# One mixing stage, three edits: products of f taken one size at a time, v turned in the group of a token with itself, pooling maps split a step in advance

## The chip, the core and the metric

The kernel runs on one core of one Trainium2 chip. What is compared is the device time of one execution in microseconds. TensorE is PE below, its weight loads PEld, VectorE is DVE, ScalarE is ACT, GpSimd is POOL, and SP is the engine whose queue issues the DMAs.

## The reference, cut to what matters

One decoder layer over 1024 tokens of width 1024: a feed-forward half step, a mixing stage, a second feed-forward half step, an added embedding, a last norm. The change lies in the mixing stage. There, `h @ w_in` is cut into the parts q, f, input (v below), output gate, pooling input and two merge gates. Branch A is a gated linear recurrence with 8 heads of 128 x 128 state; branch B takes trailing means over 2, 4, 8 and 16 positions in four channel groups, and maps each group by a 128 x 128 matrix.

```python
f = lb + (1.0 - lb) * sigmoid(f_r);  k = 1.0 - f;  q = silu(q_r);  v = i_r
S_t = diag(f_t) @ S_{t-1} + outer(k_t, v_t);   o_t = S_t.T @ q_t      # per head
o = rmsnorm(o) * silu(og_r);                   y_a = o @ w_branch_a
pooled = trailing_mean(u, (2, 4, 8, 16)) - u                         # per channel group
mixed = (pooled @ pool_w) * pool_scale;        y_b = mixed @ w_branch_b
y = sigmoid(ga_r) * y_a + sigmoid(gb_r) * y_b; x = x + y @ w_out
```

## The kernel before, in words

**The work of PE.** Every large product is made of three matmuls per 128 x 512 part (lines 157, 158, 159: high by high, high by low, low by high of a split operand); such a part is called a part below, and takes PE about 0.69 us. Two neighbouring column blocks of `w_in` are multiplied together by `pair` with seven products in place of eight, 28 parts in all. For that DMA brings two weight tiles `ra` and `rb` (line 149); POOL makes three sums of them (lines 90 and 93); ACT casts each of `wah`, `wsh`, `wth`, `wd` (line 118), and DVE subtracts to get the low parts `wal`, `wsl`, `wtl` (line 119). The first two products of a pair need `wah` and `wal` alone. All these weight tiles, and `ra` and `rb` themselves, take turns in the twelve slots of the tag "w". The results go from PSUM (banks pA, pB, pC) by ACT copies and DVE adds (lines 345, 355, 358, 81) to tiles `o`, then by a sigmoid (line 764 for a merge gate) and a store to DRAM. The gates of the merge are `ga_dram` and `gb_dram`.

**Heads.** `hgrn(h, half)` is the recurrence of one head over 512 tokens, as a generator that yields where a group of its small matmuls ends. Each group is: the scores of each token with itself (line 869, for `score`, `ident` picks the diagonal, line 871); the turn (transpose) of v (line 877, copied at 879); then seven levels, for distances 1 to 64, of small matmuls (line 898), each followed by a masked copy into `score` (line 902, for the two largest distances ACT copies at 910) and a product of q and k with products of f (`mul(both, both, by)`, line 87); then the turn of k (925), the state (930, 942, 944), the outputs (953, 955), their norm (959, 168, 961), and at a later time the turn of the output (969, 970), which is put into the next half by `turns`. The products of f over 2, 4, ... 128 tokens are slices of one tile `tot`.

**Interleaving.** `among` writes the parts of the pairs and the groups of `hgrn` in one order: with `GROUPS` groups per head and n parts, so many parts come before each group that both end together. Head 7 has the pair GA4 (`gate_pair(GA, 4, ...)`), then `act_b`, which loads the eight half tiles `m` of the pooling branch and splits them (tiles `mh`, `ml`), the pair GA6, and the first `branch_b`. PE executes exactly this order (it is written by hand). On the other engines, and on SP, a scheduler orders the instructions ahead of time, and each engine keeps its order. All loads and stores below go through the one queue of SP, in order; an SP instruction that waits for data holds up those behind it. Slots of a tag are handed out in the order of the program.

**Two more places.** `v_load` brings v of the next half, `v_next`, at one of the later yields of the half before; for the first half of head 0, `v_of` loads it when it is called. `act_b` sets `behind`, so that its loads are issued behind the last store or load written before them.

Of the kernel before, what the change touches and what calls it, by code (L numbers as in the profile page):

```python
# [25 lines left out]
HALF = 512  # L26
EPS = 1e-6
LEVELS = (1, 2, 4, 8, 16, 32, 64)
# [9 lines left out]
def hybrid_block(ctx: ExitStack, tc: tile.TileContext, a: dict, out: bass.AP):  # L38
# [16 lines left out]
    nc = tc.nc  # L55
# [15 lines left out]
    def bank(tag, s=None):  # L71
        return psum.tile([P, HALF], F32, tag=tag, name=name(s or tag), bufs=BANKS[tag])
# [13 lines left out]
    def mul(o, x, y):  # L86
        nc.vector.tensor_tensor(o, x, y, ALU.mult)  # L87
# [40 lines left out]
    def hilo_half(src, tag, s):  # L128

        t = t_(tag, s, F32R)  # L130
        n = src.shape[1]
        hi, lo = t[:, :n], t[:, HALF : HALF + n]
        split(src, hi, lo)
        return hi, lo
# [17 lines left out]
    def store(dst, src):  # L152
        latest[0] = nc.sync.dma_start(out=dst, in_=src).ins

    def mm3(ps, ah, al, bh, bl, first, last):
        kw = {"skip_group_check": True}
        nc.tensor.matmul(ps, ah, bh, start=first, stop=False, **kw)  # L157
        nc.tensor.matmul(ps, ah, bl, start=False, stop=False, **kw)  # L158
        nc.tensor.matmul(ps, al, bh, start=False, stop=last, **kw)  # L159

    def chunks(t, n=4):
        return [t[:, c * P : (c + 1) * P] for c in range(n)]
# [646 lines left out]
    def pool_maps():  # L809

        r = t_("h", "pwr")
        load(r.rearrange("p (g d) -> p g d", g=NG), a["pool_w"].rearrange("g c d -> c g d"))
        wh, wl = hilo_half(r, "w", "pwhl")
        while pooled:
            g, u = pooled.pop(0)
            gc = slice(g * P, (g + 1) * P)
            for half in range(2):
                ph, pl = hilo_half(u[half], "w", "pb")
                ps = bank("aux")
                mm3(ps, wh[:, gc], wl[:, gc], ph, pl, True, True)  # L820
                nc.scalar.mul(u[half], ps, pscale[:, g : g + 1])
                store(m_dram[g][half], u[half])
                yield False

    def pool_pair(g):
        got = {}
# [26 lines left out]
    def hgrn(h, half):  # L853

        qk, f = heads[h][0][half], heads[h][1][half]
        q, k = qk[:, L], qk[:, R]  # L860
        qc, kc = chunks(q), chunks(k)
        state = states.get(h)
        sc = scores[half]
        nc.scalar.activation(k, f, AF.Copy, scale=-1.0, bias=1.0)
        v = v_of(h, half)

        ps = bank("aux")
        for p_, k_, q_ in zip(chunks(ps), kc, qc):
            nc.tensor.matmul(p_, k_, q_, start=True, stop=True)
        yield  # L870
        nc.vector.copy_predicated(
            sc, ident.bitcast(U32).unsqueeze(1).to_broadcast([P, 4, P]),
            ps.rearrange("p (c t) -> p c t", c=4),
        )
        ps = bank("aux")
        for p_, v_ in zip(chunks(ps), chunks(v)):
            nc.tensor.transpose(p_, v_, ident)
        yield
        nc.scalar.copy(v, ps)
        vc = chunks(v)  # L880

        tots = {1: f}
        tot = t_("h", "tot")
        at = 0
        for hh in LEVELS:
            n = HALF // (2 * hh)
            pv = tots[hh].rearrange("p (a two) -> p a two", two=2)
            tots[2 * hh] = tot[:, at : at + n]
            mul(tots[2 * hh], pv[:, :, 0], pv[:, :, 1])
            at += n  # L890
        mul(q, q, f)
        for hh in LEVELS:
            n = 64 // hh
            ps = bank("aux").rearrange("p (c x) -> p c x", c=4)
            m = 64 if hh == 64 else P
            for c in range(4):
                right = qc[c].rearrange("p (a two h) -> p a two h", two=2, h=hh)[:, :, 1, :]
                nc.tensor.matmul(ps[:m, c, :64], kc[c][:, :m], right, start=True, stop=True)  # L898
            yield
            if hh < 32:  # L900
                s4 = sc.rearrange("p c (a two h) -> p c a two h", two=2, h=hh)[:, :, :, 1, :]
                nc.vector.copy_predicated(
                    s4,
                    masks[hh].bitcast(U16).unsqueeze(1).unsqueeze(3).to_broadcast([P, 4, n, hh]),
                    ps[:, :, :64].rearrange("p c (a h) -> p c a h", h=hh),
                )
            else:
                for a_ in range(n):
                    rows = slice(2 * hh * a_, 2 * hh * a_ + hh)
                    nc.scalar.copy(  # L910
                        sc[rows, :, 2 * hh * a_ + hh : 2 * hh * (a_ + 1)],
                        ps[rows, :, hh * a_ : hh * (a_ + 1)],
                    )

            na = HALF // (2 * hh)
            both = view(qk, hh, [[HALF - hh, 2], [2 * hh, na], [1, hh]])
            by = view(tots[hh], 0, [[1, 2], [2, na], [0, hh]])
            mul(both, both, by)

        need = 4 - half
        ps = bank("aux")
        for p_, a_ in zip(chunks(ps)[:need], kc):
            nc.tensor.transpose(p_, a_, ident)
        yield
        nc.scalar.copy(k[:, : need * P], ps[:, : need * P])
        ps = bank("aux")
        for p_, a_, b_ in zip(chunks(ps)[:need], kc, vc):
            nc.tensor.matmul(p_, a_, b_, start=True, stop=True)  # L930
        yield
        assert (h, half) in og_there
        og = load(t_("h", "og"), og_dram[h][half], True)
        og_last[0] = latest[0]
        befores = []

        for c, (s_, p_) in enumerate(zip(chunks(f), chunks(ps))):
            befores.append(state)
            if c == need:
                break  # L940
            if state is None:
                nc.vector.tensor_copy(s_, p_)
            else:
                nc.vector.scalar_tensor_tensor(
                    s_, state, tots[128][:, c : c + 1], p_, ALU.mult, ALU.add
                )
            state = s_
        states[h] = state

        ps = bank("aux")  # L950
        for c, p_ in enumerate(chunks(ps)):
            s_ = befores[c]
            nc.tensor.matmul(p_, sc[:, c, :], vc[c], start=True, stop=s_ is None)
            if s_ is not None:
                nc.tensor.matmul(p_, qc[c], s_, start=False, stop=True)
        yield
        rs = const.tile([P, 4], F32, tag="rso", name=name("rso"), bufs=2)
        for c, (o_, p_) in enumerate(zip(qc, chunks(ps))):
            nc.scalar.activation(o_, p_, AF.Square, accum_out=rs[:, c : c + 1])
        rstd(rs, rs, P)  # L960
        nc.vector.tensor_tensor(
            q.rearrange("p (c t) -> p c t", c=4), ps.rearrange("p (c t) -> p c t", c=4),
            rs.unsqueeze(2).to_broadcast([P, 4, P]), ALU.mult,
        )

        def turn():
            ps = bank("aux")
            for p_, a_ in zip(chunks(ps), qc):
                nc.tensor.transpose(p_, a_, ident)
            nc.vector.scalar_tensor_tensor(og, ps, onorm[:, h : h + 1], og, ALU.mult, ALU.mult)  # L970
            store(o_dram[h][half], og)

        turns.append(turn)


    GROUPS = 2 * 13
    turns = []

    def head(h):

        for half in range(2):
            for i, _ in enumerate(hgrn(h, half)):
                if i == 2 and turns:
                    turns.pop(0)()
                if i == 7:
                    at = 2 * h + half + 1
                    if at < 2 * HEADS:
                        v_next.append(v_load(at // 2, at % 2))
                yield
# [37 lines left out]
    def act_b():  # L1027
        behind[0] = latest[0]
        for g in range(NG):
            m = t_("q", "m")  # L1030
            for half, c in enumerate((L, R)):
                load(m[:, c], m_dram[g][half])
            m_parts.append(halves(hilo(m, "a", "m")))
        m_last, behind[0] = latest[0], None
        yield True
        behind[0] = m_last
        yield True
# [14 lines left out]
    with tc.manual_schedule(engines={nc.tensor.engine}):  # L1052
        for h in range(HEADS):
            its = more[h]() if h in more else (v_pair(h + 1), qf_pair(h + 1), og_pair(h + 1))
            among(its, head(h), (74 if h == 7 else 3 * PAIR + 4 * (h in (0, 2))))
        turns.pop(0)()
    behind[0] = og_last[0]

# [241 lines left out]
```

## Time and profile before

| | |
|---|---|
| time, median of 3 runs (lowest to highest) | 2426.27 us (2423.11 to 2428.93) |
| the profiled execution, its own time | 2433.22 us |
| its span, first to last instruction | 2431.5 us |
| granted clock of PE over the span | 0.986 |
| PE busy | 2332.4 us, 96% of the span |
| DVE, ACT, POOL busy | 1471.6, 979.2, 443.6 us |
| heads of the mixing stage in the trace | about 783 to 1440 us |

The busy shares are means over the whole span. The change is in one stage, so the stage's own rows are what to read: how long PE stands idle there, what it waits for, and at which clock it runs after such a wait. Lines of "waits" name the line and tile that waits, then what ended the wait, then the sum, the number and the longest of them. A row of the timeline is start, length, engine, line, operation, output <- input, shape, count, and in brackets the idle time before it and what ended it.

### The profile page before, as it was taken

The page shows a single profiled execution, that of the slowest core. Times are in us where ns is not written, and L with a number is a line of the kernel's source. Part 1 is how long each engine was busy: PE and PEld are TensorE (multiplying, and loading weights), DVE is VectorE, ACT ScalarE, POOL GpSimd, SP SyncE. Part 2 cuts the span into 40 slices and gives each one's busy share as a digit, 9 for nine tenths or more (in the row PEclk, how much of TensorE's full clock was granted, in tenths as well). Part 3 has the DMA queues.
Part 4 walks back from the last instruction along what each step waited for, and adds up shares of the span by engine and source line. Part 5 has one row for each costly group of instructions (what it writes and reads, how often), then busy time and mean ns, then how long its engine had stood idle before and what let it go on. Part 6 is the DMA issues. An engine that isn't in the chain of part 4 may idle for free.

```text
span 2431.5 us, 29305 instructions
## 1 busy us (share of the span) xinstructions
PE 2332.4 (96%) x11003; PEld 1915.3 (79%) x11003; DVE 1471.6 (61%) x2019; ACT 979.2 (40%) x1520; POOL 443.6 (18%) x390
## 2 busy tenths in 40 slices
PE   7999999999999999999999999998999999999997
PEld 5788788888877888788888877776787888888885
DVE  5655554567656766766566566677544544568558
ACT  7533333333554333333333343247333333334655
POOL 2222222200021222122222102102222232100000
PEclk9999999999999999999999999999999999999998
DMA  5243554483332222222222267652234523664323
GB/s 191 91 160 133 179 169 143 144 328 125 118 113 70 79 95 83 74 87 78 84 91 74 87 201 243 229 195 102 96 131 141 174 97 109 237 228 133 111 95 132
DMA packets 133614, 331.21 MB, mean 136 GB/s; under 512 B 15200, under 2 KB 16224, under 8 KB 133472
## 3 DMA queue, kind: packets, MB, share of 16 engines
q1 hardware_dynamic: 133472, 329.34, 39.5%
q8 instruction: 86, 1.41, 0.3%
q14 instruction: 56, 0.46, 0.1%
HBM read 228.10 MB, written 101.19 MB: 135 GB/s over the span
## 4 chain that ended last, share of the span: by engine, by line
PE 71%; DVE 10%; DMA 7%; ACT 4%; POOL 3%; issue 3%; SPq 1%; POOLq 0%; DVEq 0%; ACTq 0%
PE pA L157 11%; PE pA L159 11%; PE pA L158 11%; PE pB L157 5%; PE pB L158 5%; PE pB L159 5%; PE aux L898 3%; PE pC L158 3%; PE pC L159 3%; PE pC L157 3%; PE aux L158 2%; PE aux L159 2%; PE aux L157 2%; DMA rb<-in_ffn_w_dram 1%; DVE qk L87 1%
## 5 line engine op out<-in xcount | busy, mean ns | idle before, releaser
L90 POOL TENSOR_TENSOR s<-rb 128x512 f32<-128x512 f32 x74 | 99.5, 1345 | 815.1 <-DMA rb<-in_ffn_w_dram 408.7
L119 DVE TENSOR_TENSOR wtl<-rb,wth 128x1024 fp32r<-128x1024 f32 x74 | 90.6, 1225 | 149.2 <-ACT wth L118 149.2
L118 ACT CAST wsh<-s 128x1024 fp32r<-128x1024 f32 x74 | 77.8, 1052 | 223.3 <-POOL s L93 210.8
L93 POOL TENSOR_TENSOR rb<-ra,s 128x512 f32<-128x512 f32 x74 | 97.2, 1314 | 352.5 <-DVE wd L119 325.8
L118 ACT CAST wth<-rb 128x1024 fp32r<-128x1024 f32 x74 | 77.7, 1049 | 184.1 <-POOL rb L93 184.1
L119 DVE TENSOR_TENSOR wsl<-s,wsh 128x1024 fp32r<-128x1024 f32 x74 | 90.7, 1226 | 99.9 <-ACT wsh L118 99.9
L898 PEld LDWEIGHTS aux<-qk 128*128 128x128 f32 (+1 forms) x896 | 110.0, 187 | 37.9 <-issue 11.1
L119 DVE TENSOR_TENSOR wal<-ra,wah 128x1024 fp32r<-128x1024 f32 x74 | 91.4, 1237 | 78.5 <-PE pC L158 45.5
L118 ACT CAST gh<-gr 128x1024 fp32r<-128x1024 f32 x84 | 81.8, 981 | 141.1 <-PE aux L158 86.3
L119 DVE TENSOR_TENSOR gl<-gr,gh 128x1024 fp32r<-128x1024 f32 x84 | 94.8, 1132 | 66.9 <-ACT gh L118 66.7
L157 PE MATMUL pA<-xT1h,wsh 128*128 128x512 f32 x280 | 115.2, 411 | 18.1 <-ACT xT1h L118 14.8
L898 PE MATMUL aux<-qk 128*128 128x64 f32 (+1 forms) x896 | 111.1, 267 | 17.1 <-DVE qk L87 8.4
L157 PE MATMUL pA<-xT3h,wth 128*128 128x512 f32 x296 | 120.0, 406 | 7.2 <-ACT g L355 7.0
L118 ACT CAST wah<-ra 128x1024 fp32r<-128x1024 f32 x74 | 77.7, 1050 | 119.2 <-DMA ra<-in_ffn_w_dram 102.1
L157 PE MATMUL pB<-xT1h,wsh 128*128 128x512 f32 x296 | 119.8, 405 | 2.7 <-DVE g L81 1.2
L157 PE MATMUL pA<-x0h,wah 128*128 128x512 f32 x296 | 118.6, 401 | 2.2 <-ACT wah L118 0.9
L157 PE MATMUL pB<-x,wth 128*128 128x512 f32 x296 | 118.3, 400 | 0.0
L157 PE MATMUL pC<-x0h,wah 128*128 128x512 f32 x296 | 118.2, 399 | 0.0
L158 PE MATMUL pB<-xT1l,wsh 128*128 128x512 f32 x296 | 117.1, 396 | 0.8 <-DVE xT1l L119 0.8
L159 PE MATMUL pB<-xT1h,wsl 128*128 128x512 f32 x296 | 117.0, 395 | 0.0
L158 PE MATMUL pA<-x0l,wah 128*128 128x512 f32 x296 | 115.9, 392 | 0.8 <-DVE x0l L119 0.8
L159 PE MATMUL pA<-x0h,wal 128*128 128x512 f32 x296 | 116.2, 393 | 0.1
(347 smaller groups left out, 6593.4 us busy)
## 6 DMA issues: line engine op xcount, KB each, us to landing
ra<-in_ffn_w_dram SPq DMA_DIRECT2D x46, 512.0 KB, 3.7
rb<-in_ffn_w_dram SPq DMA_DIRECT2D x44, 512.0 KB, 3.7
gsS<-gs SPq DMA_DIRECT2D x88, 256.0 KB, 2.1
rB<-in_ffn_w_dram SPq DMA_DIRECT2D x40, 512.0 KB, 7.0
gr<-gsS SPq DMA_DIRECT2D x40, 512.0 KB, 3.5
gsA<-g SPq DMA_DIRECT2D x66, 256.0 KB, 2.0
gr<-gsA SPq DMA_DIRECT2D x30, 512.0 KB, 5.1
ra<-in_w_in_dram SPq DMA_DIRECT2D x27, 512.0 KB, 3.6
```

The source lines that it names most:

```text
L87: nc.vector.tensor_tensor(o, x, y, ALU.mult)
L90: nc.gpsimd.tensor_tensor(o, x, y, ALU.add)
L93: nc.gpsimd.tensor_tensor(o, x, y, ALU.subtract)
L118: nc.scalar.copy(hi, src)
L119: nc.vector.tensor_tensor(lo, src, hi.bitcast(F32), ALU.subtract)
L157: nc.tensor.matmul(ps, ah, bh, start=first, stop=False, **kw)
L158: nc.tensor.matmul(ps, ah, bl, start=False, stop=False, **kw)
L159: nc.tensor.matmul(ps, al, bh, start=False, stop=last, **kw)
L898: nc.tensor.matmul(ps[:m, c, :64], kc[c][:, :m], right, start=True, stop=True)
```

## The change

`hgrn`: the transposes of v are written directly behind the matmuls of each token with itself, in the same group, so a half has eleven groups and not twelve; `mul(q, q, f)` follows at once; each product of f is written behind the level that uses the one before it. The yields at which the output's turn and the load of v are written are counted accordingly (1 and 6), and `GROUPS` goes from 26 to 24: a head of 84 parts has 3.5 parts per group, not 3.23. `pool_maps`: the split of the next map's input is written ahead of the matmuls of this one, with one more yield (and n larger by one in heads 0 and 2). `act_b`: the second and fourth tile `m` come from the tag "w" and not from "q", which spares two slots of "q".

```diff
--- before.py
+++ after.py
@@ -811,16 +811,19 @@
         r = t_("h", "pwr")
         load(r.rearrange("p (g d) -> p g d", g=NG), a["pool_w"].rearrange("g c d -> c g d"))
         wh, wl = hilo_half(r, "w", "pwhl")
-        while pooled:
-            g, u = pooled.pop(0)
+        todo = [(g, half, u[half]) for g, u in pooled for half in range(2)]
+        pooled.clear()
+        parts = [hilo_half(todo[0][2], "w", "pb")]
+        yield False
+        for i, (g, half, u) in enumerate(todo):
             gc = slice(g * P, (g + 1) * P)
-            for half in range(2):
-                ph, pl = hilo_half(u[half], "w", "pb")
-                ps = bank("aux")
-                mm3(ps, wh[:, gc], wl[:, gc], ph, pl, True, True)
-                nc.scalar.mul(u[half], ps, pscale[:, g : g + 1])
-                store(m_dram[g][half], u[half])
-                yield False
+            if i + 1 < len(todo):
+                parts.append(hilo_half(todo[i + 1][2], "w", "pb"))
+            ps = bank("aux")
+            mm3(ps, wh[:, gc], wl[:, gc], *parts.pop(0), True, True)
+            nc.scalar.mul(u, ps, pscale[:, g : g + 1])
+            store(m_dram[g][half], u)
+            yield False
 
     def pool_pair(g):
         got = {}
@@ -867,27 +870,19 @@
         ps = bank("aux")
         for p_, k_, q_ in zip(chunks(ps), kc, qc):
             nc.tensor.matmul(p_, k_, q_, start=True, stop=True)
+        pv = bank("aux")
+        for p_, v_ in zip(chunks(pv), chunks(v)):
+            nc.tensor.transpose(p_, v_, ident)
         yield
+        nc.scalar.copy(v, pv)
+        vc = chunks(v)
         nc.vector.copy_predicated(
             sc, ident.bitcast(U32).unsqueeze(1).to_broadcast([P, 4, P]),
             ps.rearrange("p (c t) -> p c t", c=4),
         )
-        ps = bank("aux")
-        for p_, v_ in zip(chunks(ps), chunks(v)):
-            nc.tensor.transpose(p_, v_, ident)
-        yield
-        nc.scalar.copy(v, ps)
-        vc = chunks(v)
 
         tots = {1: f}
         tot = t_("h", "tot")
-        at = 0
-        for hh in LEVELS:
-            n = HALF // (2 * hh)
-            pv = tots[hh].rearrange("p (a two) -> p a two", two=2)
-            tots[2 * hh] = tot[:, at : at + n]
-            mul(tots[2 * hh], pv[:, :, 0], pv[:, :, 1])
-            at += n
         mul(q, q, f)
         for hh in LEVELS:
             n = 64 // hh
@@ -916,6 +911,10 @@
             both = view(qk, hh, [[HALF - hh, 2], [2 * hh, na], [1, hh]])
             by = view(tots[hh], 0, [[1, 2], [2, na], [0, hh]])
             mul(both, both, by)
+            na, at = HALF // (2 * hh), HALF - HALF // hh
+            pv = tots[hh].rearrange("p (a two) -> p a two", two=2)
+            tots[2 * hh] = tot[:, at : at + na]
+            mul(tots[2 * hh], pv[:, :, 0], pv[:, :, 1])
 
 
 
@@ -973,16 +972,16 @@
         turns.append(turn)
 
 
-    GROUPS = 2 * 13
+    GROUPS = 2 * 12
     turns = []
 
     def head(h):
 
         for half in range(2):
             for i, _ in enumerate(hgrn(h, half)):
-                if i == 2 and turns:
+                if i == 1 and turns:
                     turns.pop(0)()
-                if i == 7:
+                if i == 6:
                     at = 2 * h + half + 1
                     if at < 2 * HEADS:
                         v_next.append(v_load(at // 2, at % 2))
@@ -1027,7 +1026,7 @@
     def act_b():
         behind[0] = latest[0]
         for g in range(NG):
-            m = t_("q", "m")
+            m = t_(("q", "w")[g % 2], "m")
             for half, c in enumerate((L, R)):
                 load(m[:, c], m_dram[g][half])
             m_parts.append(halves(hilo(m, "a", "m")))
@@ -1052,7 +1051,7 @@
     with tc.manual_schedule(engines={nc.tensor.engine}):
         for h in range(HEADS):
             its = more[h]() if h in more else (v_pair(h + 1), qf_pair(h + 1), og_pair(h + 1))
-            among(its, head(h), (74 if h == 7 else 3 * PAIR + 4 * (h in (0, 2))))
+            among(its, head(h), (74 if h == 7 else 3 * PAIR + 5 * (h in (0, 2))))
         turns.pop(0)()
     behind[0] = og_last[0]
 
```

The number of instructions of each engine is the same. What moves is shown at three places.

PE at the start of head 0 (qk_5429 is the first half's q and k, v_5946 its v; pA_5981 before and pA_5986 now are the first product of the pair that follows). Before:

```order
L159 MATMUL pA_5645<-xT3h_5731,wtl_5867 128x512
L869 MATMUL aux_5948<-qk_5429 128x128 x4
L157 MATMUL pA_5981<-x0h_5171,wah_5959 128x512
L158 MATMUL pA_5981<-x0l_5172,wah_5959 128x512
L159 MATMUL pA_5981<-x0h_5171,wal_5960 128x512
...
L159 MATMUL pA_5981<-x0h_5231,wal_5960 128x512
L877 MATMUL aux_5996<-ident,v_5946 128x128 x4
L157 MATMUL pC_5982<-x0h_5171,wah_5959 128x512
```

And now (line 872 is the old 869, 875 the old 877, 893 the old 898):

```order
L159 MATMUL pA_5645<-xT3h_5731,wtl_5867 128x512
L872 MATMUL aux_5948<-qk_5429 128x128 x4
L875 MATMUL aux_5953<-ident,v_5946 128x128 x4
L157 MATMUL pA_5986<-x0h_5171,wah_5964 128x512
L158 MATMUL pA_5986<-x0l_5172,wah_5964 128x512
L159 MATMUL pA_5986<-x0h_5171,wal_5965 128x512
...
L159 MATMUL pA_5986<-x0h_5231,wal_5965 128x512
L893 MATMUL aux_6004<-qk_5429 128x64 x4
L157 MATMUL pC_5987<-x0h_5171,wah_5964 128x512
```

The transposes of v stood behind four parts, and stand directly behind the matmuls of each token with itself. The load of v is in both orders the row directly behind the load ra of the second pair, in SP's queue.

SP near the end of head 7 (ra_10627 and rb_10633 before, ra_10633 and rb_10639 now, are the weights of the pair GA6; ga_dram_1_118 is the store of the pair GA4's last gate; og is the output gate of the second half). Before:

```order
L149 DMA ra_10627<-in_w_in_dram 128x1024
L153 DMA ga_dram_1_114_241<-o_10196 128x512
L153 DMA o_dram_1_104_231<-og_10326 128x512
L149 DMA rb_10633<-in_w_in_dram 128x1024
L153 DMA ga_dram_0_115_242<-o_10386 128x512
L153 DMA ga_dram_0_113_240<-o_10197 128x512
L153 DMA ga_dram_1_112_239<-o_10195 128x512
L153 DMA ga_dram_1_118_245<-o_10388 128x512
L149 DMA m_10595<-m_dram_0_171_298 128x512
L149 DMA m_10595<-m_dram_1_172_299 128x512
L149 DMA m_10602<-m_dram_0_173_300 128x512
L149 DMA m_10602<-m_dram_1_174_301 128x512
```

And now:

```order
L153 DMA ga_dram_1_118_245<-o_10393 128x512
L149 DMA m_10601<-m_dram_0_171_298 128x512
L149 DMA m_10601<-m_dram_1_172_299 128x512
L149 DMA m_10608<-m_dram_0_173_300 128x512
L149 DMA m_10608<-m_dram_1_174_301 128x512
L149 DMA m_10615<-m_dram_0_175_302 128x512
L149 DMA m_10615<-m_dram_1_176_303 128x512
L149 DMA m_10622<-m_dram_0_177_304 128x512
L149 DMA m_10622<-m_dram_1_178_305 128x512
L149 DMA ra_10633<-in_w_in_dram 128x1024
L149 DMA og_10908<-og_dram_1_90_217 128x512
L149 DMA rb_10639<-in_w_in_dram 128x1024
```

The load ra has moved from seven rows ahead of that store to the ninth row behind it, and rb from four rows ahead to the eleventh row behind; all eight loads of m are now ahead of both. On PE the first matmul with wah (cast from ra) stands in both orders directly behind the last product of GA4.

DVE at the same place, from the norm of half 14 on to the first levels of half 15 (qk_9771 before and qk_9776 now are its q and k, `ident` marks its first masked copy). Before:

```order
L168 TENSOR_SCALAR rso_10694<-rso_10694 128x4
L961 TENSOR_TENSOR qk_9770<-aux_10677,rso_10694 128x512
L119 TENSOR_TENSOR ml_10599<-m_10595,mh_10598 128x1024
L871 COPY_PREDICATED score_5422<-ident,aux_10703 128x512
L119 TENSOR_TENSOR ml_10606<-m_10602,mh_10605 128x1024
L81 TENSOR_TENSOR o_10623<-o_10623,pA_10651 128x512
L87 TENSOR_TENSOR qk_9771<-qk_9771,f_9773 128x512
L902 COPY_PREDICATED score_5422<-mask_73,aux_10743 128x256
```

And now:

```order
L168 TENSOR_SCALAR rso_10691<-rso_10691 128x4
L960 TENSOR_TENSOR qk_9775<-aux_10674,rso_10691 128x512
L119 TENSOR_TENSOR ml_10605<-m_10601,mh_10604 128x1024
L119 TENSOR_TENSOR ml_10612<-m_10608,mh_10611 128x1024
L879 COPY_PREDICATED score_5422<-ident,aux_10700 128x512
L119 TENSOR_TENSOR ml_10619<-m_10615,mh_10618 128x1024
L119 TENSOR_TENSOR wd_10648<-rb_10639,wd_10648 128x512
L119 TENSOR_TENSOR ml_10626<-m_10622,mh_10625 128x1024
L81 TENSOR_TENSOR o_10629<-o_10629,pA_10657 128x512
L119 TENSOR_TENSOR wtl_10654<-rb_10639,wth_10653 128x1024
L87 TENSOR_TENSOR qk_9776<-qk_9776,f_9778 128x512
L897 COPY_PREDICATED score_5422<-mask_73,aux_10727 128x256
```

The weights' wtl of GA6 stood above this piece and now stands ahead of half 15's first product with f; the products of f of half 15 stand above the piece in both.

DVE in the first half of head 1 (qk_6147 before, qk_6146 now; tot_6960 and tot_6945 are the products of f of the half that follows). Before:

```order
L902 COPY_PREDICATED score_5421<-mask_81,aux_6730 128x64x4
L87 TENSOR_TENSOR qk_6147<-qk_6147,tot_6677 128x2x64x4
L87 TENSOR_TENSOR tot_6960<-f_6150 128x256
L87 TENSOR_TENSOR tot_6960<-tot_6960 128x128
L87 TENSOR_TENSOR tot_6960<-tot_6960 128x64
L87 TENSOR_TENSOR tot_6960<-tot_6960 128x32
L81 TENSOR_TENSOR o_6428<-o_6428,pB_6549 128x512
L87 TENSOR_TENSOR tot_6960<-tot_6960 128x16
L119 TENSOR_TENSOR wsl_6835<-s_1297_6831,wsh_6834 128x1024
L902 COPY_PREDICATED score_5421<-mask_85,aux_6753 128x32x8
L87 TENSOR_TENSOR qk_6147<-qk_6147,tot_6677 128x2x32x8
```

And now:

```order
L87 TENSOR_TENSOR tot_6945<-f_6149 128x256
L897 COPY_PREDICATED score_5421<-mask_81,aux_6717 128x64x4
L87 TENSOR_TENSOR qk_6146<-qk_6146,tot_6668 128x2x64x4
L87 TENSOR_TENSOR tot_6945<-tot_6945 128x128
L87 TENSOR_TENSOR tot_6945<-tot_6945 128x64
L87 TENSOR_TENSOR tot_6945<-tot_6945 128x32
L87 TENSOR_TENSOR tot_6945<-tot_6945 128x16
L87 TENSOR_TENSOR tot_6945<-tot_6945 128x8
L87 TENSOR_TENSOR tot_6945<-tot_6945 128x4
L897 COPY_PREDICATED score_5421<-mask_85,aux_6736 128x32x8
L87 TENSOR_TENSOR qk_6146<-qk_6146,tot_6668 128x2x32x8
```

The seven products of the following half stood on both sides of the 32x8 level, with wsl ahead of it; now the six later ones stand together behind the level before it, and wsl behind the 32x8 level.

## The prediction

> **What bounds the kernel now.** I read the page first, for the engine that sets the time.
>
> ```profile
> span 2431.5 us, 29305 instructions
> PE 2332.4 (96%) x11003; PEld 1915.3 (79%) x11003; DVE 1471.6 (61%) x2019; ACT 979.2 (40%) x1520; POOL 443.6 (18%) x390
> PE 71%; DVE 10%; DMA 7%; ACT 4%; POOL 3%; issue 3%; SPq 1%; POOLq 0%; DVEq 0%; ACTq 0%
> ```
>
> PE is busy for 96%, and the chain that ended last lies on it for 71%. The number of matmuls doesn't change, so the change can win or lose only where PE stands idle or runs at a lower clock. Hence next the windows of the changed stage (stretch and its length; busy time of PE, PEld, DVE, ACT, POOL; granted clock; DMA), the whole of it and short stretches around its idle times, and then what PE waits for there.
>
> ```profile
> 783.00:1440.00 657.00, 635.59 (x3498) 534.44 (x3498) 418.93 (x716) 242.63 (x480) 137.46 (x104) 0.99 0.27 89
> 886.60:890.00 3.40, 1.97 (x13) 1.44 (x11) 2.64 (x7) 1.22 (x2) 0.00 (x0) 1.00 0.21 77
> 890.00:893.40 3.40, 3.40 (x11) 2.73 (x10) 1.02 (x2) 0.00 (x0) 0.00 (x0) 0.51 0.00 0
> 991.60:1011.00 19.40, 15.30 (x83) 12.04 (x82) 19.04 (x48) 5.02 (x9) 0.00 (x0) 1.00 0.16 54
> 1012.90:1019.70 6.80, 6.71 (x23) 5.87 (x23) 3.21 (x5) 2.42 (x4) 1.52 (x2) 0.50 0.62 220
> 1063.90:1067.30 3.40, 3.40 (x22) 3.01 (x22) 1.11 (x3) 0.00 (x0) 0.00 (x0) 1.00 0.00 0
> 1419.10:1425.90 6.80, 6.20 (x20) 5.36 (x21) 3.68 (x6) 1.79 (x3) 0.00 (x0) 0.50 0.68 237
> ```
> ```profile
> PE aux L898 <- DVE qk L87: 8.4, 13, 1.3
> PE aux L898 <- DVE tot L87: 4.2, 3, 1.4
> PE aux L898 <- ACT wb L118: 3.1, 1, 3.1
> PE aux L158 <- DVE pb L119: 2.4, 1, 2.4
> PE pA L157 <- ACT o L358: 1.1, 1, 1.1
> ```
>
> Of 657 us PE is idle for 657.00 - 635.59 = 21.4. Three stretches of 3.4, 6.8 and 6.8 us run at half the clock, each behind an idle time; half of their length is lost, 1.7 + 3.4 + 3.4 = 8.5 us. So 29.9 us is all that could be won here, 1.2% of the kernel. A third wait of about the same length as the first, 1.36 us, cost no clock (the stretch at 1063.9 has 1.00).
>
> **Products of f, one size at a time; GROUPS 24.** What a level costs DVE:
>
> ```profile
> L87 DVE TENSOR_TENSOR qk<-qk,tot 128x512 f32<-128x512 f32 x96 | 77.9, 811 | 29.3 <-PE aux L898 29.1
> L902 DVE COPY_PREDICATED score<-mask,aux 128x256 f32<-128x256 uint16 x80 | 44.3, 553 | 56.2 <-PE aux L898 56.1
> L871 DVE COPY_PREDICATED score<-ident,aux 128x512 f32<-128x512 uint32 x16 | 11.8, 737 | 0.0
> L87 DVE TENSOR_TENSOR tot<-f 128x256 f32<-128x256 f32 x16 | 9.9, 619 | 0.1
> 889.15 1.12 PE L898 MATMUL aux<-qk 128*128 128x64 f32 x8 [1.43 <-DVE tot L87]
> ```
>
> The 1.43 us ahead of 889.15 is a level whose product on DVE was late: between it and the one before stood products of f, an add and wsl. In the new order wsl is behind that level and the first product of f ahead of the level before; so the three waits on tot, 4.2 us, go, with the 1.7 us of clock behind the first. The 13 waits on qk hold 8.4 us. A part is 0.69 us, so a group of 3.5 parts instead of 3.23 covers 0.19 us more. By walking the new order with these durations I let the two longest of halves 9 and 13 go (2.8 us with what follows them), and 2.2 of the small ones; 3.4 remain, mostly in halves 1 and 5, where DVE also makes the trailing means. New waits come up: with v's group gone, only three or four parts lie between a token's scores with itself and the first level, where six or seven lay, and the chain (copy by ident, product with f, 0.74 + 0.81 us, behind other DVE work) ends 0.3 us behind PE in the even halves. I take 2.1 us for all, and 0.6 more in half 5. Between 0 and 5 us are possible: 8 halves by 0.6.
>
> Each small group also breaks the flow of large matmuls:
>
> ```profile
> 885.39 0.48 PE L157 MATMUL pA<-xT1h,wsh 128*128 128x512 f32 x1
> 885.70 0.39 PE L158 MATMUL pA<-xT1l,wsh 128*128 128x512 f32 x1
> 885.93 0.40 PE L159 MATMUL pA<-xT1h,wsl 128*128 128x512 f32 x1
> ```
>
> The first behind a group takes 0.31 us until the next starts, others 0.23. Sixteen groups fewer: 16 x 0.085 = 1.4 us. Together: -4.2 - 1.7 - 5.0 - 1.4 + 2.1 + 0.6, about -9.5 us (-5 to -13).
>
> **Maps split a step ahead.** The 2.4 us on pb, with 3.4 us of clock behind it, looks like its gain. But DVE, busy for 19.04 of the 19.40 us from 991.6 to 1011, works off means, levels and splits one after another there, and the same instructions still come before. I put it at 0: the wait moves by a group. From both sides: -5.8 if it goes, +1 if the earlier split holds up a level.
>
> **v turned at once, first half.** All other v are loaded five groups or so ahead of their half, and at 657 / 16 / 11 = 3.7 us each that is some 18 us. The first is not:
>
> ```profile
> 782.26 1.29 POOL L93 TENSOR_TENSOR rb<-ra,s 128x512 f32<-128x512 f32 x1 [4.00 <-DVE wd L119]
> 783.52 1.05 PE L869 MATMUL aux<-qk 128*128 128x128 f32 x8
> 783.58 0.33 SPq L149 DMA_DIRECT2D ra<-in_w_in_dram  x1
> 783.96 0.42 SPq L149 DMA_DIRECT2D v<-v_dram  x1
> 784.33 0.48 PE L157 MATMUL pA<-x0h,wah 128*128 128x512 f32 x1
> 787.73 0.66 PE L877 MATMUL aux<-ident,v 128*128 128x128 f32 x4 [0.42 <-DMA v<-v_dram]
> ```
>
> Its load is issued directly behind ra, which waits for a slot until POOL is done (782.26 + 1.29 = 783.55). That stays. v is there at 787.7, and PE will now ask for it at 784.33: 3.4 us idle where 0.42 was, so +2.95, and the four parts between come later. Behind 1.43 and 2.38 us of idle time the clock was halved for 3.4 and 6.8 us, so 1.7 to 3.4 us more: +4.6 to 6.4, I take 5.5. [...]
>
> **m in the tag "w", end of head 7.** This is the term that decides. E is 1399.66, where GA4's last product ends and GA6's first starts, with wah of ra.
>
> ```profile
> 1371.35 0.33 SPq L149 DMA_DIRECT2D ra<-in_w_in_dram  x1
> 1399.66 0.39 PE L157 MATMUL pA<-x0h,wah 128*128 128x512 f32 x1
> 1402.16 0.64 ACT L764 ACTIVATE o<-o 128x512 f32<-128x512 f32 x1 [0.92 <-DVE o L81]
> 1402.82 0.32 SPq L153 DMA_DIRECT2D ga_dram<-o  x1
> 1403.19 1.86 SPq L149 DMA_DIRECT2D m<-m_dram  x4
> 1409.00 1.06 ACT L118 CAST mh<-m 128x1024 fp32r<-128x1024 f32 x1 [1.08 <-DMA m<-m_dram]
> 1413.04 1.08 PE L898 MATMUL aux<-qk 128*128 128x64 f32 x8 [0.57 <-ACT o L764]
> 1419.70 1.94 PE L898 MATMUL aux<-qk 128*128 128x64 f32 x8 [3.06 <-ACT wb L118]
> ```
> ```profile
> ra<-in_w_in_dram SPq DMA_DIRECT2D x22, 512.0 KB, 3.6
> L90 POOL TENSOR_TENSOR s<-rb 128x512 f32<-128x512 f32 x22 | 29.3, 1333 | 229.2 <-DMA rb<-in_w_in_dram 186.3 <-PE aux L159 17.4 <-PE aux L925 13.7
> L119 DVE TENSOR_TENSOR wsl<-s,wsh 128x1024 fp32r<-128x1024 f32 x74 | 90.7, 1226 | 99.9 <-ACT wsh L118 99.9
> ```
>
> Before, ra was issued 28 us ahead of its use. Now it stands behind the store of GA4's last gate, which waits for that very product (copy, add, sigmoid: issued at E + 3.2 before, 2.3 by my estimate where ACT is free), and behind eight loads of m at 1.86 / 4 = 0.47 us of issue each: 2.3 + 0.3 + 3.8 = E + 6.4. Alone it would take 3.6 us, so E + 10; behind 2 MB of m it takes longer, and were it to take twice as long it would be E + 13.5; I take 11.5, nearer the fast end since m lands while ra is issued. One cast, 1.06, and PE resumes at E + 12.6. It has nothing else to do: the order is fixed.
>
> A second wait follows. The new DVE row has wal, wsl, four ml, wd and wtl ahead of half 15's first product with f. rb lands two rows later, E + 13.5; two sums on POOL (1.35 each) and a cast give wsh at 17.3; then DVE in its order: wsl 1.23, the norm of half 14 with its step on POOL 2.0, two ml 2.5, the copy by ident 0.74, ml 1.23, wd 0.7, ml 1.23, an add 0.7, wtl 1.23, the product 0.81: E + 29.7. PE gets there at 12.6 + 0.8 (wal) + nine parts 6.2 + three groups 2.7 = 22.3, up to 25 where it waits for wd. Before it was at 1413.04, E + 13.4. PE has then done three parts fewer (2.1 us), and what came next before, 3.1 us for wb, 3.4 of clock and 1.1 at 1436 (the wait on o), is mostly covered; new dips cost 1.7 to 3.4. So 29.7 + 2.1 - 13.4 - 7.6 + 2.5 = +13.3 us. The ends: with the second wait hidden and no dip +4, with slow DMAs +19.
>
> **Sum.** -9.5 + 0 + 5.5 + 13.3 = +9.3 us on the profiled 2433.2. That run lies 7 us above the median, 2426.3; put on the median it makes 2435.3 us (the likeliest one's own range 2428 to 2443).
>
> **Rivals.** (1) Only the gains: the loads are there in time, or the SP queue lets ra through. -9.5 and the old tail's waits partly gone: 2411 to 2420. For it: in every other pair ra lands long ahead. Against it: the fixed row of SP. It decides where ra is issued before E - 5. (2) Faster after all, by the maps: if the early split takes the pb wait away, -5.8 in head 2, and with a tail at its low end (+4): -9.5 - 5.8 + 5.5 + 4, 2420. Against it: DVE without a gap. (3) A draw: the first stall of the tail, its second hidden since the level's DVE work gets done meanwhile: -9.5 + 4.6 + 6, 2427. For it: PE has nine parts and three groups to do after it resumes. (4) More: both tail waits with slow m, 2445 to 2449. (5) The edits do nothing: 2426; excluded nearly by the rows of the order. (6) The clock stays full behind the first stall: without the 2.5 us for its dip, 2432.8, a case inside the forecast, about 0.1 of its 0.52, since two shorter idle times had dips.
>
> **Chances.** Forecast 0.52, (1) 0.08, (2) 0.05, (3) 0.20, (4) 0.12, (5) 0.03. A measurement can tell 0.2%, 4.9 us: bounds 2421.4 and 2431.1. Faster: (1) and (2), 0.13. Same: (3), (5) mostly 0.21. Slower: the forecast nearly whole and (4), 0.66 with what (3) reaches over. The range leaves out (1) and the upper half of (4): 2420 to 2446.
>
> **What would show it.** In the changed trace: an idle time of 3.4 us ahead of v's transposes near 784; ra of GA6 issued behind eight m; PE idle for 10 to 13 us at about 1393 for wah, then waits of 4 to 7 up to half 15's first level; no waits on tot. I am wrong if ra goes out early, if PE finds wah within 5 us, or if the chain through half 15 is hidden.

## The result, and the profile after

The change makes the kernel slower by 1.1%: 2453.4 us (median of 4 runs, 2448.4 to 2457.8) against 2425.5 us, ratio 1.0107 with a 95% interval of 1.0093 to 1.0122, so about 26 us (0.0107 times 2426). The prediction was 2435.3 us, in a range of 2420 to 2446. The direction was right; the loss is nearly three times the 9.3 us forecast.

The page after, first lines:

```profile
span 2456.1 us, 29284 instructions
PE 2334.3 (95%) x11003; PEld 1917.6 (78%) x11003; DVE 1485.6 (60%) x2019; ACT 981.4 (40%) x1520; POOL 441.1 (18%) x390
```

PE's busy time is 2 us longer than before (2332.4), its matmuls are the same in number, and the span is 24.6 us longer: in these two executions nearly all of the loss is idle time of PE. The waits of PE in the heads, up to GA6's first product (which stands at 1399.66 before and behind 1403.81 after):

```profile
PE aux L893 <- DVE qk L87: 9.5, 14, 0.8
PE aux L875 <- DMA v<-v_dram: 3.4, 1, 3.4
PE aux L158 <- DVE pb L119: 3.3, 1, 3.3
PE aux L954 <- DVE f L943: 1.3, 2, 0.7
PE aux L893 <- DVE pw L87: 1.3, 2, 0.7
PE aux L893 <- ACT f L717: 0.3, 1, 0.3
```

Without v that is 15.7 us. Before, the same stretch held 8.4 + 4.2 + 2.4 on qk, tot and pb, and 0.8 on the cast pb, together 15.8. No wait on tot is left, as forecast, but the time is not won: the same three levels, the fifth of halves 2, 6 and 10 (counted from 0), still wait 0.80, 0.79 and 0.79 us, now on qk, and new waits have come up elsewhere. The start of head 0 is as forecast too (timeline):

```profile
783.98 1.29 POOL L93 TENSOR_TENSOR rb<-ra,s 128x512 f32<-128x512 f32 x1 [3.57 <-DVE wd L119]
785.24 1.05 PE L872 MATMUL aux<-qk 128*128 128x128 f32 x8
785.29 0.33 SPq L149 DMA_DIRECT2D ra<-in_w_in_dram  x1
785.67 0.43 SPq L149 DMA_DIRECT2D v<-v_dram  x1
789.73 0.66 PE L875 MATMUL aux<-ident,v 128*128 128x128 f32 x4 [3.44 <-DMA v<-v_dram]
```

The end of head 7, in order of time (E is now 1403.81, where PE falls idle):

```profile
1405.00 0.32 SPq L153 DMA_DIRECT2D ga_dram<-o  x1
1405.37 3.76 SPq L149 DMA_DIRECT2D m<-m_dram  x8
1409.23 0.50 SPq L149 DMA_DIRECT2D ra<-in_w_in_dram  x1
...
1415.65 1.04 ACT L118 CAST wah<-ra 128x1024 fp32r<-128x1024 f32 x1 [10.68 <-DMA ra<-in_w_in_dram]
1416.75 0.80 PE L157 MATMUL pA<-x0h,wah 128*128 128x512 f32 x1 [12.94 <-ACT wah L118]
...
1424.92 0.17 DVE L168 TENSOR_SCALAR rso<-rso 128x4 f32<-128x4 f32 x1 [2.14 <-ACT qk L958]
1426.22 0.69 DVE L960 TENSOR_TENSOR qk<-aux,rso 128x512 f32<-128x512 f32 x1 [1.13 <-POOL rso L169]
1426.83 2.35 DVE L119 TENSOR_TENSOR ml<-m,mh 128x1024 fp32r<-128x1024 f32 x2
...
1431.67 2.12 POOL L93 TENSOR_TENSOR rb<-ra,s 128x512 f32<-128x512 f32 x1 [5.48 <-DVE wd L119]
...
1434.90 1.23 DVE L119 TENSOR_TENSOR wtl<-rb,wth 128x1024 fp32r<-128x1024 f32 x1 [1.64 <-ACT wth L118]
1436.04 0.68 DVE L87 TENSOR_TENSOR qk<-qk,f 128x512 f32<-128x512 f32 x1
1436.87 1.94 PE L893 MATMUL aux<-qk 128*128 128x64 f32 x8 [7.68 <-DVE qk L87]
```

The load ra goes out behind the store and eight m, PE is idle for 12.94 us, and after 12 us of work it is idle again for 7.68 us, at half 15's first level. A third wait, of 2.17 us, stands further on; before, 0.6 us were waited there:

```profile
1524.83 0.50 PE L157 MATMUL pB<-xT1h,wsh 128*128 128x512 f32 x1 [2.17 <-ACT xT1h L118]
```

Behind each of the three comes a dip, as a stretch at half the clock is called here. The windows of PE's clock (columns as in the prediction):

```profile
1405.80:1416.10 10.30, 0.00 (x0) 0.00 (x0) 0.00 (x0) 0.45 (x1) 0.00 (x0) 0.50 0.99 341
1416.10:1422.90 6.80, 6.11 (x18) 4.72 (x19) 2.45 (x2) 1.64 (x2) 3.93 (x3) 0.50 0.06 23
1422.90:1426.30 3.40, 3.40 (x23) 3.02 (x23) 0.25 (x2) 2.54 (x10) 1.02 (x1) 1.00 0.00 0
1436.50:1443.30 6.80, 6.43 (x21) 5.60 (x22) 3.33 (x6) 1.11 (x2) 0.00 (x0) 0.50 0.51 177
1525.30:1532.10 6.80, 6.04 (x15) 4.76 (x15) 4.98 (x6) 1.85 (x3) 0.00 (x0) 0.50 0.56 176
```

PE works 6.11 + 6.43 + 6.04 = 18.6 us at half the clock behind E; half of it, 9.3 us, is lost, in part where PE would have waited anyhow. Before, one dip stood there, with 6.20 us of work.

### The profile page after: what moved, and what is told of

Read it like the earlier page. It is cut to its first block, busy times and chain, and to the rows that moved or that the text cites. A ratio compares the mean times of both kernels' runs of the same rounds, so it can differ in the third digit from the quotient of the medians.

```text
span 2456.1 us, 29284 instructions
## 1 busy us (share of the span) xinstructions
PE 2334.3 (95%) x11003; PEld 1917.6 (78%) x11003; DVE 1485.6 (60%) x2019; ACT 981.4 (40%) x1520; POOL 441.1 (18%) x390
```

## The experiments

Twelve kernels, each compared with the kernel before in runs on the same chip. Its own median was 2425 to 2428 us in these comparisons, so the ratios are what to compare; 0.1% is 2.4 us.

| kernel | ratio to before | 95% interval | us, of 2426 |
|---|---|---|---|
| the change | 1.0107 | 1.0093 to 1.0122 | +26.0 |
| after_mq | 1.0025 | 1.0015 to 1.0035 | +6.1 |
| before_mw | 1.0066 | 1.0049 to 1.0084 | +16.0 |
| after_ra_first | 1.0062 | 1.0047 to 1.0076 | +15.0 |
| ra_first_q | 1.0010 | 1.0000 to 1.0020 | +2.4 |
| after_mq_v0 | 0.9996 | 0.9987 to 1.0005 | -1.0 |
| rfq_v0 | 0.9982 | 0.9971 to 0.9994 | -4.4 |
| before_tots | 1.0004 | 0.9992 to 1.0016 | +1.0 |
| before_vt_v0 | 1.0010 | 0.9999 to 1.0021 | +2.4 |
| before_pm | 1.0001 | 0.9990 to 1.0012 | +0.2 |
| v0_opm | 1.0002 | 0.9990 to 1.0013 | +0.5 |
| v0_notots | 0.9963 | 0.9951 to 0.9976 | -9.0 |
| v0_pooltots | 0.9968 | 0.9955 to 0.9980 | -7.8 |

**The tag of m, undone and alone.** The changed kernel with the old line, and the old kernel with the new line:

```diff
-            m = t_(("q", "w")[g % 2], "m")
+            m = t_("q", "m")
```

> The changed kernel with all four tiles m in the tag q again, as before; the load ra of GA6 is again seven rows ahead of the store of GA4's last gate. Theory 1 (the late ra is what costs): the idle time of 12.9 us ahead of GA6 and the one of 7.7 us at half 15's first level go, with 3.2 + 3.4 us of half clock behind them, and the old tail's waits of about 5 and 3.4 of clock come back: some 20 us less than the changed kernel, 2430 to 2435. Theory 2 (the loss is spread over the heads, in new waits of 0.5 to 0.8 us): at most 6 us less, 2447 or more.

> The kernel before with the second and fourth tile m in the tag w, nothing else. ra and rb of GA6 go behind the store and the eight loads of m here too. Theory 1: 18 to 22 us slower than before, 2444 to 2448, with an idle time of 11 to 14 us ahead of GA6's first product. Theory 2: that the late ra hurts only with the new order of the groups (four fewer), less than 8 us, under 2434.

after_mq takes 0.82% off the changed kernel, 20 us (22.7 by the medians, 2453.4 and 2430.7): theory 1. before_mw loses 0.66%, 16 us (12 to 20), a little less than expected and far more than theory 2 allows. Its waits of PE show the same two idle times as the changed kernel, 13.5 us for wah and 5.0 us at half 15's first level:

```profile
PE pA L157 <- ACT wah L118: 13.5, 1, 13.5
PE aux L898 <- DVE qk L87: 13.0, 14, 5.0
```

So this one line is worth 60 to 80% of the whole loss, in the old order of groups as in the new one.

**ra ahead of m.** In the changed kernel, ra and rb of GA6 are loaded at the start of act_b and handed to the pair; the loads of m are then issued behind rb and not behind the store:

```diff
     def act_b():
+        for s, j in (("ra", 6), ("rb", 7)):
+            ga6.append(load(t_("w", s), w_in[GA + j], True))
         behind[0] = latest[0]
```

> The changed kernel with ra and rb of GA6 loaded in act_b ahead of the loads of m; m stays in q and w by turns. The loads of m then stand behind rb and not behind the store. Theory 1 (what costs is ra standing behind the store and m): the idle time ahead of GA6 is under 1 us, 2425 to 2434. Rival (two slots fewer of w for the weights cost by themselves): PE still waits for weights of GA6 for 5 us or more, 2440 or more.

The first idle time is gone, and yet 1.0062 remains: I had expected the whole loss to go. Theory 1 is right for the first wait and wrong for the second, and part of the rival holds. Waits of PE and timeline of after_ra_first:

```profile
PE aux L893 <- DVE qk L87: 16.4, 14, 7.7
1411.75 0.62 ACT L118 CAST wd<-rb 128x512 fp32r<-128x512 f32 x1 [0.52 <-DVE ml L119]
1414.21 2.11 POOL L93 TENSOR_TENSOR rb<-ra,s 128x512 f32<-128x512 f32 x1 [5.48 <-DVE wd L119]
1419.41 1.94 PE L893 MATMUL aux<-qk 128*128 128x64 f32 x8 [7.67 <-DVE qk L87]
```

rb has been there for 20 us and more (POOL read it at 1390.28). wd waits for ml. As I read it, wd takes the slot of w that a tile m gives back when ml has read it; no row shows the slots themselves, and the next kernel tests it. The last sum of POOL waits for wd, wtl for that sum, and half 15's first product stands behind wtl on DVE. The same kernel with all m in q:

> As after_ra_first (ra and rb of GA6 loaded ahead of m), but all four tiles m in q. DVE then has wd and wtl of GA6 above the norm of half 14 again, and two ml, not four, ahead of half 15's first product. Theory (in after_ra_first the 7.7 us at half 15 came from m holding two slots of w, so that wd waited until ml had read m): that wait is 3 us or less, 2426 to 2433, as after_mq. Rival (the loads of m ahead of the store, and the order of ra and rb, caused it): a wait of 6 us or more, 2437 to 2443.

PE's waits on qk in ra_first_q:

```profile
PE aux L893 <- DVE qk L87: 10.3, 14, 1.3
```

ra_first_q is at 1.0010, and its longest wait on qk is 1.3 us in place of 7.7. So the loss of the tail has two halves: ra behind m on SP, 0.45%, 11 us (6 to 16; 1.0107 to 1.0062), and m in the slots of the weights, 0.52%, 13 us (8 to 17; 1.0062 to 1.0010). Their sum, 24 us, is the whole step from the changed kernel to ra_first_q. It is not the 20 us (16 to 24) of after_mq, since in ra_first_q the loads of m stand behind rb and not behind the store, but the intervals overlap.

**v in head 0's first half.** after_mq with one group more, in that half alone, so that the transposes of v stand behind four parts again:

```diff
+        if (h, half) == (0, 0):
+            yield
         pv = bank("aux")
```

> As after_mq, and in head 0's first half alone the transposes of v stand a group behind the scores again. Theory 1: the idle time of 3.4 us ahead of them goes back to about 0.4, with no clock to win since none was lost there: 3 us less than after_mq. Rival (the time is lost again at the next wait, since DVE or the loads set it): less than 1 us.

> As ra_first_q, with the transposes of v in head 0's first half a group later, as in after_mq_v0. Theory: 5 to 7 us less than ra_first_q (3.1 of idle time and, in most executions, a dip), 2419 to 2427; against before from 0.3% faster to the same. Rival: m's first tiles on SP hold up the stores and loads behind them, 2428 or more.

after_mq_v0 is 0.29%, 7.0 us faster than after_mq; rfq_v0 is 0.28%, 6.8 us faster than ra_first_q (each 3 to 10 us by the intervals). The wait on v is 0.3 and 0.8 us. I had expected 3 us in the first case, since the changed kernel's profile shows no half clock there. Four profiled executions hold this stall, 3.3 to 3.5 us long: the changed kernel and after_ra_first without a dip, after_mq and ra_first_q with one (the first fence is after_mq, the second ra_first_q):

```profile
784.00:787.40 3.40, 0.37 (x4) 0.18 (x2) 2.94 (x4) 1.85 (x4) 0.00 (x0) 1.00 0.72 231
787.40:790.80 3.40, 3.08 (x10) 2.60 (x11) 2.26 (x9) 1.33 (x2) 0.00 (x0) 0.50 0.21 77
```
```profile
785.40:788.80 3.40, 1.27 (x10) 1.04 (x8) 2.03 (x3) 1.71 (x3) 0.26 (x1) 1.00 0.59 174
788.80:792.20 3.40, 2.13 (x7) 1.91 (x8) 3.16 (x10) 2.09 (x3) 0.00 (x0) 0.50 0.36 134
792.20:795.60 3.40, 3.40 (x9) 2.64 (x8) 0.00 (x0) 0.00 (x0) 0.00 (x0) 0.50 0.00 0
```

One execution lost 1.5 us of clock behind this stall (half of 3.08), one 2.8 (half of 2.13 + 3.40), the two others none. With the 3 us of idle time these make 3 to 6 us; the 7 us of the ratios have these in their interval.

**Each other part alone.** before_tots, before_pm and before_vt_v0 are the old kernel with one of the change's parts as in its diff (before_vt_v0 with the extra group of head 0); v0_opm is after_mq_v0 with the old pooling maps.

> The kernel before with the products of f written one size at a time, nothing else. In the built order only DVE changes, and there only in the first half of four heads, where the product of q with f moves two or three rows ahead; the products of the other halves had been put ahead by the scheduler and stay where they were. Theory 1 (this edit does nearly nothing, and the three waits on tot stay): within 3 us of before. Theory of the prediction (the waits on tot and the dip behind them go with it): 4 to 6 us faster.

> The kernel before with v turned in the group of the scores and GROUPS 24, but in head 0's first half a group later, as before. Theory 1 (this edit alone holds what the heads win and lose; waits of 0.6 to 0.8 us at the first and fifth levels take the place of those removed): from 4 us faster to 2 us slower. Theory of the prediction (waits on tot go, first levels wait for 0.3 us each): 7 us or more faster.

> The kernel before with the pooling maps split a step in advance, nothing else. Prediction: 0, the wait on pb only moves. Rival 1 (the split goes ahead of levels that PE waits for, and the maps' first split is later by a level): 1 to 4 us slower, with the wait on pb at 3.3 us as in the changed kernel. Rival 2 (the wait on pb goes): 4 to 6 us faster.

> after_mq_v0 with the pooling maps as before, so products of f, v's turn and GROUPS alone. If the split in advance costs 1 to 4 us in the changed kernel too, this is 1 to 4 us faster than after_mq_v0, the wait on pb is 2.4 us or less, and it beats before by 0 to 5 us; if it costs nothing, the same as after_mq_v0 within 1.5 us.

None differs from before: +1.0, +2.4, +0.2 and +0.5 us, all with 1 in the interval. The products of f, written one size at a time, alone change next to nothing: PE's waits on tot in before_tots stand as they were,

```profile
PE aux L891 <- DVE tot L87: 4.1, 3, 1.4
```

since the scheduler had put them among the levels of the half before, whatever their place in the program. They go with v's turn and GROUPS, but then PE waits on qk for longer up to 1390 us, 14.8 us in before_vt_v0 where the kernel before has 8.4 on qk and 4.2 on tot:

```profile
PE aux L899 <- DVE qk L87: 14.8, 15, 3.4
```

The maps split in advance leave the wait on pb at 2.4 us where they stand alone (before_pm); with the new groups it is 3.3 us with the split (after_mq_v0) and 2.4 without (v0_opm). They cost or win nothing that these runs can tell: v0_opm is 0.06% behind after_mq_v0, within the intervals.

**Why the heads' gain went.** Two kernels on the base of after_mq_v0. v0_notots leaves out the products of f (each level multiplies by a slice of f itself); v0_pooltots has POOL make them:

```diff
# v0_notots
-            tots[2 * hh] = tot[:, at : at + na]
-            mul(tots[2 * hh], pv[:, :, 0], pv[:, :, 1])
+            tots[2 * hh] = f[:, at : at + na]
# v0_pooltots
-            mul(tots[2 * hh], pv[:, :, 0], pv[:, :, 1])
+            nc.gpsimd.tensor_tensor(tots[2 * hh], pv[:, :, 0], pv[:, :, 1], ALU.mult)
```

> As after_mq_v0, but the products of f are left out: each level multiplies q and k with a slice of f itself, so 112 DVE instructions, 35 us, are gone. Theory 1 (the block of products that the scheduler puts ahead of the fifth level is what makes that level late): the waits of 0.8 us at the fourth and fifth levels and of 1.5 us in half 14 go, those of 0.6 to 0.7 us at the first levels stay; 3 to 6 us less than after_mq_v0. Theory 2 (the chain of copy and product by itself is what PE waits for): at most 2 us less. Theory of the prediction would have all that in the changed kernel already.

> As after_mq_v0, with the products of f made by POOL, which is idle for four fifths of the heads. Theory 1 (DVE's time is what counts): 2 to 5 us less than after_mq_v0. Rival (POOL's work slows DVE, whose product took 1.72 us and not 0.69 beside a POOL sum, and POOL's own order holds up the weights' sums): the same or up to 10 us more.

v0_notots is 0.33%, 8 us faster than after_mq_v0, v0_pooltots 0.28%, 6.8 us; more than theory 1 said for each, but the intervals (4 to 12 and 3 to 11 us) reach into its ranges. PE's waits on qk up to 1390 us in v0_notots:

```profile
PE aux L894 <- DVE qk L87: 8.0, 11, 1.4
```

after_mq_v0 has 10.3 in 16 there and 1.5 on tot. The 0.77 to 0.79 us at the fifth levels of halves 2, 6 and 10 are gone. Those of 0.64 to 0.69 at the first levels stay, as does one of 0.80 at half 12's fourth, and half 6's first level waits 1.36 us in place of 0.54. So the products do make the fifth levels late, and the timeline of the changed kernel says how:

```profile
887.58 0.68 DVE L87 TENSOR_TENSOR qk<-qk,tot 128x512 f32<-128x512 f32 x1
888.13 1.28 POOL L90 TENSOR_TENSOR s<-rb 128x512 f32<-128x512 f32 x1 [13.27 <-DMA rb<-in_w_in_dram]
888.18 4.51 DVE L87 TENSOR_TENSOR tot<-tot 128x128 f32<-128x128 f32 x6
889.49 1.29 POOL L93 TENSOR_TENSOR s<-s,ra 128x512 f32<-128x512 f32 x1
890.74 1.30 POOL L93 TENSOR_TENSOR rb<-ra,rb 128x512 f32<-128x512 f32 x1
892.61 0.42 DVE L897 COPY_PREDICATED score<-mask,aux 128x256 f32<-128x256 uint16 x1
893.77 1.08 PE L893 MATMUL aux<-qk 128*128 128x64 f32 x8 [0.80 <-DVE qk L87]
```

Six small products take 4.51 us, because POOL makes its three sums of rb at that moment. Taken one by one, the first three start at 888.18, 889.60 and 890.89 and end at 889.56, 890.86 and 892.08, each just behind the end of a sum of POOL (889.41, 890.78, 892.04); the last three, alone, take 0.18, 0.17 and 0.16. The first three so took 1.38, 1.26 and 1.19 us, where they take 0.29, 0.22 and 0.19 in head 0's first half. The same six products take 4.5 us in halves 6 and 10 too, beside POOL's sums, and 1.2 us in sum in the eleven halves where no sum runs beside them. That v0_pooltots wins fits this: there the products are POOL's, and DVE is busy for 402.9 of the 657 us from 783 on, against 433.1 in after_mq_v0; no run parts the time that DVE is spared from the time that POOL's sums no longer take from it.

The kernel before had the same in another place, ahead of its wait of 1.43 us on tot:

```profile
882.29 1.72 DVE L87 TENSOR_TENSOR qk<-qk,tot 128x512 f32<-128x512 f32 x1
883.94 1.50 DVE L87 TENSOR_TENSOR tot<-f 128x256 f32<-128x256 f32 x1
```

POOL's sums ran from 882.18 to 885.16. The first product, 128x256, took 0.40 to 0.43 us in thirteen halves and 1.50 to 1.52 in three, just ahead of the three waits on tot; the prediction's row for it, 619 ns on average, mixes the two. So the change moved which DVE instructions POOL's sums hold up.

v0_pooltots is the version to keep: 2421.8 us, 0.32% faster than the kernel before (0.20 to 0.45%) and 1.4% faster than the change.

## Why the prediction was wrong, point by point

Two terms of the sum failed, the gain of the heads and the loss of the tail.

- **Products of f and GROUPS, -9.5 us forecast, -1.0 measured** (after_mq_v0, -3.2 to +1.2). This is the first step that failed: waits were taken away without a price for what comes in their place. I walked the new order with mean durations; where the products now stand, six of them share the time with POOL's sums and take 4.5 us and not 1.2, so the three fifth levels still wait, for 2.4 us in all in place of 4.2. The new waits at the first levels I had in kind: five of 0.54 to 0.69 us, 3.2 in sum, forecast 2.7. Not forecast at all were the waits at the fourth levels of halves 0, 4, 8 and 12, 2.7 us, and of the outputs on the state (L954 on f), 1.3 us; for part of these the cause stays open, since those of halves 4 and 12 stand in v0_notots too. What the prediction credits to the products' new place did not come from it: by themselves they change +1.0 us and leave 4.1 us on tot (before_tots). The 1.7 us for the dip at 890 was no fixed price of that wait: before and before_pm have a dip there, before_mw and before_tots, with waits of 1.36 and 1.37 us, none. The 1.4 us for the seams can't be seen apart.
- **Maps split ahead, 0 forecast, 0 measured.** Right; the wait on pb did not go, and grew from 2.4 to 3.3 us in the changed kernel's profile.
- **v at once, +5.5 forecast (4.6 to 6.4), +7 measured** (0.28 and 0.29% in two pairs). Right in place and kind, and within the intervals (3 to 10 us) in size. The idle time was 3.44, forecast 3.4. The dip behind it, forecast at 1.7 to 3.4 us and left out in rival (6), came in two of four executions.
- **m in "w", +13.3 forecast (4 to 19), +20 measured (16 to 24).** This is the second step that failed. The first wait was right: PE resumed at E + 12.94, forecast 12.6. Some luck is in that number, since ra was issued earlier than forecast, at E + 5.4 and not 6.4, and took longer to land, 6.4 us and not 5.1. The second wait was there, 7.68 us (forecast 4.7 to 7.4). What failed is the chain's end, E + 29.7 where E + 33.1 was measured, and the term for the clock, +2.5. The chain: half 14's outputs ran on PE for the most part inside the first dip, and DVE waited 2.14 us for them, so that the norm ended at 1426.91, E + 23.1, where I had 20.5, and everything behind it on DVE came later. I had also walked DVE's row without a gap, but wtl waits for the cast of POOL's last sum, 1.64 us; that sum took 2.12 us beside DVE's work, not 1.3. The clock: one dip costs what I took, 1.7 to 3.4 us, but there were three. The first is the one that makes the chain late; the two behind the chain's end lose half of 6.43 and of 6.04 us, 6.2 in all, and the wait of 2.2 us ahead of the third I had not foreseen (after_ra_first has it too, the kernel before has 0.6 there). With these two figures the prediction's own sum reads 33.1 + 2.1 - 13.4 - 7.6 + 6.2 = +20.4. after_ra_first shows that the second wait had also a cause I had not named: wd waits there until ml has read m.
- **Sum.** By the runs -1 + 0 + 7 + 20 = +26. That this is the measured difference is no check, since the steps lie end to end from before over after_mq_v0 and after_mq to the change. The parts measured on the old kernel are a better one: +16.0, +2.4, +1.0 and +0.2 (before_mw, before_vt_v0, before_tots, before_pm), with the 7 for v, make 26.6. Of the 16.7 us missing in the forecast, 8.5 are the heads' gain, 6.7 the tail and 1.5 v. Put on the median, -9.5 + 5.5 + 13.3 is 2435.6 and not 2435.3, a slip of 0.3. Rival (4), both tail waits at length, came nearest, and its upper end was still too low since it carried the same -9.5.

## What to carry to other kernels

A tile put into another tag takes its turn ahead of whatever takes that tag's slots next: see which loads and weights stand behind it in the queue before counting the slots that it frees. A wait that is read from a trace and taken away is a gain only when the next work on that engine is priced with what runs beside it there, not with its mean: a mean may mix two cases, as 0.41 and 1.5 us did here. Behind each long idle time of PE a possible stretch at half clock belongs in the sum (it came behind 12.94, 7.68 and 2.17 us here, and behind 3.3 to 3.5 us in two of four executions), and in the chain of the engine that waits for PE's results.

## What the runs showed of the hardware

- A small product on DVE, 0.2 to 0.3 us alone, took as long as the POOL sum beside it, 1.2 to 1.4 us beside sums of 1.28 to 1.30 (the changed kernel, 888.18 to 892.08), one per sum.
- The stretches at half clock were 3.4 us long (the kernel before, at 890.0), 6.8 (there at 1012.9 and 1419.1), 10.2 (the changed kernel, 1433.1 to 1443.3) and 17.1 (there 1405.8 to 1422.9, of which 10.3 are idle). In the changed kernel the starts at 1405.8, 1433.1 and 1525.3 lie 27.3 and 92.2 us apart, 8 and 27 times 3.41. A stall of 3.3 to 3.5 us in one place of the program gave a dip of 0, 0, 3.4 and 6.8 us in four executions. A stretch of 3.40 us in which PE was busy for 1.27 stood ahead of a dip (785.4 above), and one with 1.97 before, at 886.6. Stretches with 1.69 and 1.67 us in the changed kernel, from 784.6 on, were followed by none, so the busy time of one such stretch alone does not decide it; what does stays open.
